# Sliding-window attention scores in half blocks: 64 queries of two heads against 192 keys

## The chip, the cores and the metric

The kernel runs on one core of a Trainium2 chip. The core has a matrix engine (PE, with a queue of its own for weight loads, PEld), a vector engine (DVE), an activation engine (ACT), a general engine (POOL) and a queue that issues transfers (SP), beside 16 DMA engines that do them. The metric is the device time of one execution in microseconds (us); before and after are compared by the median of several executions on the same chip.

## The reference

One layer of a decoder trunk: `x` is 2048 positions by 1024 channels, everything in 32-bit floats. The layer modulates `x` by a condition vector, projects it (`u @ w_in`) into queries, keys, values, an attention gate, a pool input, a pool gate and two merge gates, runs two mixers, projects and merges them, and ends in a layer norm. What the change touches is the first mixer:

```python
N_Q_HEADS, N_KV_HEADS, HEAD_DIM, WINDOW, BLOCK = 16, 2, 64, 128, 128

q_loc = jnp.arange(BLOCK)[:, None]
k_loc = jnp.arange(2 * BLOCK)[None, :]
dist = q_loc + BLOCK - k_loc
in_window = (dist >= 0) & (dist < WINDOW)
...
logits = jnp.einsum('bnqhgd,bnkhd->bnhgqk', qb, kb) * (HEAD_DIM ** -0.5) + bias
logits = jnp.where(mask, logits, NEG_INF)
probs = jax.nn.softmax(jnp.concatenate([logits, sink], axis=-1), axis=-1)[..., :-1]
out = jnp.einsum('bnhgqk,bnkhd->bnqhgd', probs, vb)
```

A block of 128 queries sees the 128 keys before the block and its own 128. Query number q of the block may use keys q+1 to q+128 of these 256. So each query uses 128 of the 256 keys; the first 64 queries of a block together use keys 1 to 191, the last 64 use keys 65 to 255. A learned bias by distance is added, and each head has a sink, one more logit that takes part in the softmax and is then dropped.

## The kernel before, in words

The kernel is one instruction stream per engine, in an order that the program writes down ahead of time (`keep_in_program_order`): no engine reorders, and each waits at its own place in line for the semaphores of others.

**The large products.** All projections are 1024-wide matrix products done by a Strassen-like scheme: seven products in place of eight, named `B11, T1, T2, B21, T3, B22, T4` after the tile set that they stream. Each is 12 matmuls of 128x512 (`product`, `mm3`: a high and a low part of both sides, three matmuls per 128 rows). A `Quad` is one such group of seven; its weights come from HBM into `W` and `A`, POOL forms sums of them, ACT rounds them to the high part (`w_set`), DVE forms the low part. `plan` fixes which product comes when, `run` walks them, and `consume` takes a finished product away: for queries (`q_quad`, line 576) ACT writes the high part `q_hi`, DVE the low part `q_lo`, and SP stores both into `q_d` in HBM two products later. Tiles for this come from a ring `c` of 4 (first half of the sequence) or 5 (second half).

**The stages.** The sequence is handled in two halves, s = 0 and 1, of 1024 positions. Each half has a start (`g0`, `g1`: keys, values, the first two query tiles, the first gates), a stage in which attention runs between the products (`o0`, `o1`), and an end (`e0`, `e1`: the pool mixer beside the last gates). A last stage (`mix`) does the output projections and the norm.

**Attention as an overlay.** `overlay` (line 769) cuts the attention of a half into 64 steps: 8 pairs of query heads (j) by 8 blocks of 128 positions. `beat` is called after every three matmuls of a product and lets a step in at a fixed rate, about one per 4.8 us. So where a step's PE work stands between the product's matmuls is fixed by the program. Step n does, in this order:

- PE: `scores(n)`, four matmuls 128x256 into the one bank `lg` (two heads, high and low part of the keys `kk`; the weights are 128 queries of one head, `qs`); `transposes(n-2)`, four transposes 128x128 into the one bank `pt`; `values(n-3)`, four matmuls 128x256 into `pv`.
- DVE and ACT: a reciprocal of the softmax sums of step n-1; two ACT operations that scale its probabilities by it; ACT copies `pt` to `pth` (rounded), and half of `pv` to `o`; per head, DVE adds the bias to `lg` and finds the row minimum in one operation (into the tile `L`), and ACT takes the exponential and its sum; DVE forms the low part `ptl`; two DVE adds finish the output block `st`.
- POOL: `new_l(n+1)` copies the two sinks into column 256 of each head's half of the next `L` tile (a ring of 3).

`lg` and `pt` exist once. So the scores of step n wait until DVE has read the `lg` of step n-1, and the transposes in step n wait until DVE has made the `ptl` of the step before.

**Transfers.** SP issues nearly all of them, in program order, with eight completion semaphores in turn. In the overlay it loads the queries of two blocks (`load_q`, line 796, two transfers of 128 KB) every second step, one pair ahead, and the bias of the next head pair (`load_bias`, line 805) once per 8 steps, into a tile `bt` of which there is one. The bias comes from `e_rep`, a copy of the per-head table for each of 128 partitions, read at a shifted offset per partition; `spread_bias` (line 766) writes these copies.

Of the kernel before, what the change touches and what calls it, by code (L numbers as in the profile page):

```python
# [15 lines left out]
ALU = mybir.AluOpType  # L16
# [43 lines left out]
def kernel(  # L60
# [30 lines left out]
    BF16 = mybir.dt.bfloat16  # L91
    set_names = ("B11", "T1", "T2", "B21", "T3", "B22", "T4")
# [7 lines left out]
    nsink = cp.tile([P, HEADS], F32, name="nsink")  # L100
# [7 lines left out]
    e_rep = dp.tile([P, HEADS, ET], F32, name="e_rep")  # L108
# [24 lines left out]
    q_d = dp.tile([2, KT, 2, 2, P, CH], F32, name="q_d")  # L133
# [632 lines left out]
    def spread_bias(j, q):  # L766
        q.dma_start(e_rep[:, 2 * j : 2 * j + 2, :], e_d[2 * j : 2 * j + 2, :].partition_broadcast(P))

    def overlay(ph, s, n_slots):
# [4 lines left out]
        kvt, qts, bts = {}, {}, {}  # L774
        marks, Es, Ls, pts, xs, pvs, outs, ags, kept = {}, {}, {}, {}, {}, {}, {}, {}, {}
# [20 lines left out]
        def load_q(h):  # L796
# [3 lines left out]
            q = qts[h] = tp.tile([P, 2, 2 * P], F32R, tag="qs", bufs=2, name="qs")  # L800
            for n in range(2):
                src = q_d[s, j, t, n][:, c * 2 * P : (c + 1) * 2 * P].rearrange("(h d) c -> d h c", h=2)
                sp.dma_start(as32(q[n * HD : (n + 1) * HD]), src)

        def load_bias(j):
            if j >= KT:
                return
            bt = bts[j] = tp.tile([P, 2, 2 * P], F32, tag="bt", bufs=1, name="bt")
            e_src = e_rep[:, 2 * j : 2 * j + 2, :]
            sp.dma_start(bt, bass.AP(e_src.tensor, e_src.offset + P - 1, [[HEADS * ET - 1, P], [ET, 2], [1, 2 * P]]))  # L810

        def new_l(n):
            if n < N:
                j = n // U
                room = tp.tile([P, 2 * 257 + 4], F32, tag="L", bufs=3, name="L")
                Ls[n] = room[:, 0 : 2 * 257].rearrange("p (h k) -> p h k", h=2)
                marks[n] = room[:, 2 * 257 : 2 * 257 + 2], room[:, 2 * 257 + 2 :]
                pool.tensor_copy(Ls[n][:, :, 256], nsink[:, 2 * j : 2 * j + 2])
# [4 lines left out]
        def values(n):  # L823
            k0 = k0_of(n)
            pv = pvs[n] = bank("pv")[:, 0 : 2 * P].rearrange("p (h q) -> p h q", h=2)
# [5 lines left out]
        def scores(n):  # L831
            k0, b, q = k0_of(n), n % U, qts[n // 2]
            lg = bank("lg").rearrange("p (h k) -> p h k", h=2)
            at = n % 2 * P
# [12 lines left out]
        def transposes(n):  # L847
            L = Ls.pop(n)
            pt = ps.tile([P, 2, 2, P], F32, tag="pt", bufs=1, name="pt")
            for hf in range(k0_of(n) // P, 2):  # L850
                for h in range(2):
                    pe.transpose(pt[:, hf, h, :], L[:, h, hf * P : (hf + 1) * P], ident)
# [21 lines left out]
        def step(n):  # L874
# [4 lines left out]
            if n - 1 in Es:  # L879
                E, e0, sm = Es.pop(n - 1)  # L880
                dve.reciprocal(sm, sm)
                for h in range(2):
                    act.activation(E[:, h, e0:256], E[:, h, e0:256], AF.Copy, scale=sm[:, h : h + 1])
# [10 lines left out]
            if lg is not None:  # L894
                j, e0 = n // U, k0_of(n)
                L = Ls[n]
                nm, sm = marks.pop(n)
                for h in range(2):
                    dve.tensor_tensor_reduce(
                        L[:, h, e0:256],  # L900
                        lg[:, h, e0:],
                        bts[j][:, h, e0:],
                        1.0,
                        nsink[:, 2 * j + h : 2 * j + h + 1],
                        ALU.add,
                        ALU.min,
                        nm[:, h : h + 1],
                    )
                    act.activation(
                        L[:, h, e0:257],  # L910
                        L[:, h, e0:257],
                        AF.Exp,
                        bias=nm[:, h : h + 1],
                        scale=-1.0,
                        accum_out=sm[:, h : h + 1],
                    )
                Es[n] = L, e0, sm
            if pt is not None:
                low(dve, lo[:, h0:], pt[:, h0:], hi[:, h0:])
            if o2 is not None:  # L920
# [7 lines left out]
                for h in range(2):  # L928
                    dve.tensor_tensor(
                        outs[jj, tt][h * HD : (h + 1) * HD, bb * P : (bb + 1) * P], pv[0:HD, h, :], o2[:, h, :], ALU.add  # L930
                    )
# [283 lines left out]
    def head(ph, grp):  # L1215
# [11 lines left out]

        dve.memset(as32(sets["B21"][:, 0, 0, :]), 1.0)
# [4 lines left out]
        act.dma_start(nsink, sinks.partition_broadcast(P))  # L1233
# [384 lines left out]
```

## Time and profile before

| | |
|---|---|
| median of 3 runs | 1700.26 us (1699.17 to 1703.98) |
| the profiled execution: its time, its span | 1703.35 us, 1701.2 us |
| mean granted PE clock | 0.993 |
| busy: PE, DVE, ACT, POOL | 1665.3, 1185.1, 988.4, 589.4 us |
| DMA: bytes moved, mean rate | 389.50 MB, 229 GB/s |
| the first overlay (s = 0) | about 160 to 476 us |
| the second overlay (s = 1) | about 742 to 1055 us |

Nearly every instruction goes through one helper line (`op(*args)`, line 56), so the profile's groups are told apart by tile names and shapes. `lg<-kk,qs` are the score matmuls, `pt<-ident,L` the transposes, `L<-lg,bt,nsink` the bias-and-minimum operation of DVE, `L<-L` on ACT with 257 columns the exponential and with 256 columns the scaling. With `set_...` and `w_set` as inputs a matmul belongs to a product, also where it writes `lg` or `c`. PE's busy time is modelled: an instruction counts until its results drain, so the busy time of one (`mean ns`) is longer than its share of a stream, and a stretch in which PE counts as busy may still hold short waits. The weight-load queue (PEld) shows such waits too.

### The profile page before, as it was taken

The page shows a single profiled execution, that of the slowest core. Times are in us where ns is not written, and L with a number is a line of the kernel's source. Part 1 is how long each engine was busy: PE and PEld are TensorE (multiplying, and loading weights), DVE is VectorE, ACT ScalarE, POOL GpSimd, SP SyncE. Part 2 cuts the span into 40 slices and gives each one's busy share as a digit, 9 for nine tenths or more (in the row PEclk, how much of TensorE's full clock was granted, in tenths as well). Part 3 has the DMA queues.
Part 4 walks back from the last instruction along what each step waited for, and adds up shares of the span by engine and source line. Part 5 has one row for each costly group of instructions (what it writes and reads, how often), then busy time and mean ns, then how long its engine had stood idle before and what let it go on. Part 6 is the DMA issues. An engine that isn't in the chain of part 4 may idle for free.

```text
span 1701.2 us, 24948 instructions
## 1 busy us (share of the span) xinstructions
PE 1665.3 (98%) x8112; PEld 1397.0 (82%) x8112; DVE 1185.1 (70%) x2167; ACT 988.4 (58%) x1943; POOL 589.4 (35%) x563
## 2 busy tenths in 40 slices
PE   9899999999999999999999999999999999999997
PEld 7788888888788888888888888888888888888886
DVE  6855666666647778656666666487876785778878
ACT  4645888787853336358877787333544453434553
POOL 3013454545462223323424333322242211113544
PEclk9899999999999999999999999999999999999999
DMA  9489676776557889865456454589968685777343
GB/s 358 151 294 311 202 225 217 242 239 208 170 178 223 264 288 326 289 206 157 150 171 215 156 175 135 190 280 326 329 238 309 197 312 201 261 264 281 149 149 124
DMA packets 236833, 389.50 MB, mean 229 GB/s; under 512 B 20872, under 2 KB 90528, under 8 KB 236576
## 3 DMA queue, kind: packets, MB, share of 16 engines
q1 hardware_dynamic: 231280, 382.36, 66.8%
q10 hardware_dynamic: 5392, 5.53, 1.0%
q8 instruction: 64, 1.05, 0.3%
q14 instruction: 65, 0.53, 0.1%
q0 software_dynamic: 32, 0.02, 0.0%
HBM read 243.63 MB, written 147.35 MB: 230 GB/s over the span
## 4 chain that ended last, share of the span: by engine, by line
PE 68%; ACT 11%; DVE 6%; issue 5%; DMA 3%; POOL 1%; SPq 1%; DVEq 0%; ACTq 0%; POOLq 0%
PE mm L56 43%; PE lg L56 11%; PE c L56 9%; ACT L L56 5%; PE pv L56 3%; PE pt L56 3%; DVE w_set L56 2%; ACT pth L56 2%; ACT w_set L56 1%; DVE wide L56 1%; ACT sig L56 1%; DVE p L56 1%; DVE ptl L56 1%; SPq L56 1%; ACT q_hi L56 0%
## 5 line engine op out<-in xcount | busy, mean ns | idle before, releaser
L56 PE MATMUL mm<-set_B,w_set 128*128 128x512 f32 x2664 | 652.7, 391 | 0.6 <-DVE w_set L56 0.6
L56 PEld LDWEIGHTS mm<-set_B,w_set 128*128 128x128 f32 x2664 | 496.6, 188 | 103.7 <-DVE w_set L56 1.5
L56 PE MATMUL mm<-set_T,w_set 128*128 128x512 f32 x1896 | 466.1, 392 | 1.5 <-POOL w_set L56 1.2
L56 POOL TENSOR_TENSOR W<-W 128x512 f32<-128x512 f32 x185 | 266.9, 1453 | 573.1 <-DVE w_set L56 394.0
L56 PEld LDWEIGHTS mm<-set_T,w_set 128*128 128x128 f32 x1896 | 351.5, 189 | 74.4 <-POOL w_set L56 2.5
L56 DVE TENSOR_TENSOR w_set<-W,w_set 128x1024 fp32r<-128x1024 f32 x197 | 254.5, 1292 | 110.5 <-ACT w_set L56 109.2
L56 ACT ACTIVATE L<-L 128x257 f32<-128x257 f32 (+3 forms) x512 | 241.4, 498 | 96.8 <-DVE L L56 96.3
L56 ACT CAST w_set<-W 128x1024 fp32r<-128x1024 f32 x222 | 232.2, 1047 | 97.2 <-PE mm L56 54.2
L56 PE MATMUL lg<-set_T,w_set 128*128 128x512 f32 x828 | 201.0, 391 | 2.7 <-ACT lg L56 1.7
L56 PE MATMUL c<-set_T,w_set 128*128 128x512 f32 x828 | 200.8, 391 | 0.0
L56 PEld LDWEIGHTS lg<-set_T,w_set 128*128 128x128 f32 x828 | 155.4, 188 | 36.2 <-ACT lg L56 2.1
L56 PEld LDWEIGHTS c<-set_T,w_set 128*128 128x128 f32 x828 | 155.8, 189 | 32.2
L56 DVE TENSOR_TENSOR ptl<-pt,pth 128x512 fp32r<-128x512 f32 (+1 forms) x128 | 86.4, 675 | 112.6 <-ACT pth L56 112.6
L56 POOL TENSOR_TENSOR W<-W,A 128x512 f32<-128x512 f32 x41 | 57.9, 1412 | 275.1 <-DMA A<-in_win_dram 102.7
L56 DVE CUSTOM_DVE_ANT_0 L<-lg,bt,nsink 128x256 f32<-128x256 f32 (+1 forms) x256 | 110.1, 467 | 25.1 <-PE lg L56 20.9
L56 ACT ACTIVATE sig<-mm 128x512 f32<-128x512 f32 x76 | 45.5, 599 | 94.6 <-PE mm L56 92.5
L56 PEld LDWEIGHTS lg<-kk,qs 128*128 128x128 f32 x512 | 77.4, 189 | 15.4 <-DVE L L56 4.6
L56 PE MATMUL pt<-ident,L 128*128 128x128 f32 x496 | 76.7, 276 | 9.3 <-DVE ptl L56 8.8
L56 PE MATMUL lg<-kk,qs 128*128 128x256 f32 (+1 forms) x512 | 81.5, 281 | 2.2 <-DVE L L56 1.9
L56 POOL TENSOR_TENSOR w_set<-W,w_set 128x1024 fp32r<-128x1024 f32 x25 | 61.0, 2441 | 63.7 <-ACT w_set L56 37.5
L56 PE MATMUL pv<-pth,vv 128*128 128x256 f32 x248 | 74.8, 323 | 1.1 <-DMA vv<-v_d 1.1
L56 DVE TENSOR_TENSOR st<-pv,o 64x128 f32<-64x128 f32 x256 | 71.3, 279 | 5.5 <-ACT o L56 3.8
(207 smaller groups left out, 1884.2 us busy)
## 6 DMA issues: line engine op xcount, KB each, us to landing
W<-in_win_dram SPq DMA_DIRECT2D x40, 512.0 KB, 5.8
qs<-q_d SPq DMA_DIRECT2D x128, 128.0 KB, 4.3
sums_d<-W SPq DMA_DIRECT2D x62, 256.0 KB, 4.1
W<-sums_d SPq DMA_DIRECT2D x31, 512.0 KB, 4.2
ain_d<-st SPq DMA_DIRECT2D x56, 256.0 KB, 3.5
A<-in_win_dram SPq DMA_DIRECT2D x42, 256.0 KB, 5.6
q_d<-q_hi SPq DMA_DIRECT2D x32, 256.0 KB, 4.4
q_d<-q_lo SPq DMA_DIRECT2D x32, 256.0 KB, 4.2
```

Of the source, the lines that this page charges most:

```text
L56: return lambda *args, **kw: self.tc.keep_in_program_order(op(*args, **kw))
```

## The change

Each step still handles one pair of heads and one block of 128 queries, with the same number of instructions. What lies on the 128 partitions differs: before, a score matmul had the 128 queries of one head; now it has 64 queries of both heads, first the early 64, then the late 64 (`eo` = 0, 1). For the early 64 only keys 0 to 191 are multiplied, biased and exponentiated, for the late 64 keys 64 to 255 (`span_of`). With it go:

- **Query layout.** `q_d` in HBM is now cut into pieces of 64 positions. A store (`keep_q`) writes 128 x 8 pieces of 64 numbers (256 bytes) where it wrote 128 rows of 512; a load reads 64 x 8 such pieces where it read 64 x 2 rows of 256 numbers (1 KB). The bytes are the same.
- **Bias.** A row of `bt` is now 192 numbers, the same for both halves up to a shift, for 64 partitions per head: two transfers of half the partitions, and two `bt` tiles in turn. `e_rep` has 64 copies in place of 128.
- **The L tiles** are three fixed tiles; the keys that no query of a half can use stay zero (three memsets on POOL at the start of each overlay), so that the transposes and the value matmuls keep their full width. The sinks stand in the column before the early half's keys and the column behind the late half's. `nsink` has one column per pair of heads.
- **Two more matmuls** of 128x512 (in `behind`): the bank `lg` is filled once at the start of `e0` and `e1`, as `c1` was already, since the scores no longer write all of it.

```diff
     class Pools:
         def __init__(self, name, **bufs):
             self.name, self.bufs, self.turns = name, {"c": 4, "p": 2, **bufs}, {}
-            self.fresh = True
+            self.fresh = {0, 1} if "pg" in bufs else {1}
...
-                if q.x and ph.fresh:
+                if q.pair and q.x in ph.fresh:
                     t = sets["B11"][:, 0, 0, :]
                     mm(q.c, t[:, 0:P], t, start=True, stop=True, skip_group_check=True)
-                    ph.fresh = False
+                    ph.fresh.remove(q.x)
...
+    def keep_q(dst, x):
+        sp.dma_start(dst.rearrange("b p c -> p b c"), x.rearrange("p (b c) -> p b c", c=HD))
...
-            defer(2 if m else 1, lambda: [sp.dma_start(q_d[s, m + mi, t, n], as32(x)) for n, x in enumerate((hi, lo))])
+            defer(2 if m else 1, lambda: [keep_q(q_d[s, m + mi, t, n], as32(x)) for n, x in enumerate((hi, lo))])
...
+        rooms = [tp.tile([P, 2 * 257 + 4], F32, tag=f"L{i}", bufs=1, name="L") for i in range(3)]
+        for room in rooms:
+            pool.memset(room[:, 1 + BAND : 1 + BAND + P], 0.0)
...
-            bt = bts[j] = tp.tile([P, 2, 2 * P], F32, tag="bt", bufs=1, name="bt")
-            e_src = e_rep[:, 2 * j : 2 * j + 2, :]
-            sp.dma_start(bt, bass.AP(e_src.tensor, e_src.offset + P - 1, [[HEADS * ET - 1, P], [ET, 2], [1, 2 * P]]))
+            bt = bts[j] = tp.tile([P, BAND], F32, tag="bt", bufs=2, name="bt")
+            for h in range(2):
+                e_src = e_rep[:, 2 * j + h, :]
+                at_q = bass.AP(e_src.tensor, e_src.offset + P - 1, [[HEADS * ET - 1, HD], [1, BAND]])
+                sp.dma_start(bt[h * HD : (h + 1) * HD], at_q)
...
+        def span_of(n, eo):
+            k0 = k0_of(n)
+            return (max(k0, HD), 2 * P) if eo else (k0, BAND)
...
-            for h in range(2):
+            for eo in range(2):
+                whi = q[:, n % 2 * 2 + eo].rearrange("p h c -> p (h c)")
+                k0, k1 = span_of(n, eo)
                 for hl in range(2):
                     mm(
-                        lg[:, h, k0:],
-                        q[:, h, at : at + P],
-                        kvt["k"][:, hl, (b - 1 + s) * P + k0 : (b + 1 + s) * P],
-                        start=h == 0 and hl == 0,
+                        lg[:, eo, k0:k1],
+                        whi,
+                        kvt["k"][:, hl, (b - 1 + s) * P + k0 : (b - 1 + s) * P + k1],
+                        start=eo == 0 and hl == 0,
                         stop=hl == 1,
                         skip_group_check=True,
                     )
...
-                for h in range(2):
-                    act.activation(E[:, h, e0:256], E[:, h, e0:256], AF.Copy, scale=sm[:, h : h + 1])
+                for eo in range(2):
+                    k0, k1 = span_of(n - 1, eo)
+                    x = E[:, 1 + 2 * P * eo + k0 : 1 + 2 * P * eo + k1]
+                    act.activation(x, x, AF.Copy, scale=sm[:, eo : eo + 1])
```

The order of all other instructions on every engine is as before. On SP, at the start of the first overlay, these are the rows before (rows read as: output, input, shape as partitions x pieces x numbers, and the semaphores waited for; `q_d` is the query store in HBM, `qs` the queries of two blocks, `e_rep` the bias copies, `A22`, `W` and `sums_d` weights and their kept sums):

```order
L56 DMA e_rep_77<-e_d_76 128x768 [waits DMAHW7_49,DMAHW5_49,DMASW0_49]
L56 DMA qs_1493<-q_d_89 64x2x256 [waits DMAHW6_49]
L56 DMA qs_1493<-q_d_89 64x2x256
L56 DMA q_d_89<-q_hi_1470 128x512 [waits DMAHW0_49,Activation_49]
L56 DMA q_d_89<-q_lo_1471 128x512 [waits DMAHW1_49,DVE_49]
L56 DMA A22_1515<-wmix_d_75 128x512 [waits DMAHW2_49,DVE_49]
L56 DMA sums_d_94<-W_1212 128x512 [waits DMAHW3_49,Pool_49]
L56 DMA q_d_89<-q_hi_1508 128x512 [waits DMAHW4_49,Activation_49]
```

and these are the same places now:

```order
L56 DMA e_rep_77<-e_d_76 64x768 [waits DMAHW1_49,DMAHW7_49,DMAHW0_49,DMASW0_49]
L56 DMA qs_1500<-q_d_89 64x8x64 x2
L56 DMA q_d_89<-q_hi_1477 128x8x64 [waits DMAHW2_49,Activation_49]
L56 DMA q_d_89<-q_lo_1478 128x8x64 [waits DMAHW3_49,DVE_49]
L56 DMA A22_1521<-wmix_d_75 128x512 [waits DMAHW4_49,DVE_49]
L56 DMA sums_d_94<-W_1213 128x512 [waits DMAHW5_49,Pool_49]
L56 DMA q_d_89<-q_hi_1514 128x8x64 [waits DMAHW6_49,Activation_49]
```

Nothing has changed places; the pieces of the query transfers are smaller and more, and the bias copies half as many.

On DVE, the second and third step of the first overlay read so before (`ISA` on `L<-lg,bt,nsink` is the bias-and-minimum operation, the row behind it reads its result out; `Pool_49` is POOL's sink copy into that `L`):

```order
L56 RECIPROCAL L_1496<-L_1496 128x2
L56 ISA L_1535<-lg_1567,bt_1393,nsink_71 128x256 [waits PE_49]
L56 ISA L_1535 128x1
L56 ISA L_1535<-lg_1567,bt_1393,nsink_71 128x256 [waits Pool_49]
L56 ISA L_1535 128x1
L56 TENSOR_TENSOR ptl_1579<-pt_1572,pth_1578 128x256 [waits Activation_49]
L56 RECIPROCAL L_1535<-L_1535 128x2 [waits Activation_49]
```

and now:

```order
L56 RECIPROCAL L_1389<-L_1389 128x2
L56 ISA L_1390<-lg_1572,bt_1400,nsink_71 128x192 [waits PE_49,Pool_49]
L56 ISA L_1390 128x1
L56 ISA L_1390<-lg_1572,bt_1400,nsink_71 128x192
L56 ISA L_1390 128x1
L56 TENSOR_TENSOR ptl_1584<-pt_1577,pth_1583 128x256 [waits DMAHW7_49,Activation_49]
L56 RECIPROCAL L_1390<-L_1390 128x2 [waits Activation_49]
```

The operations are a quarter narrower, and the wait for POOL's sink copy has moved from the second of the two to the first.

More of the change, by code (lines that the diff above doesn't have):

```diff
@@ L91 @@
     BF16 = mybir.dt.bfloat16
+    BAND = P + HD
     set_names = ("B11", "T1", "T2", "B21", "T3", "B22", "T4")
@@ L99 @@
     mod = cp.tile([P, 24], F32, name="mod")
-    nsink = cp.tile([P, HEADS], F32, name="nsink")
+    nsink = cp.tile([P, KT], F32, name="nsink")
     psc = cp.tile([P, KT], F32, name="psc")
@@ L107 @@
     e_d = dp.tile([HEADS, ET], F32, name="e_d")
-    e_rep = dp.tile([P, HEADS, ET], F32, name="e_rep")
+    e_rep = dp.tile([HD, HEADS, ET], F32, name="e_rep")
     gate_d = dp.tile([KT, P], F32, name="gate_d")
@@ L132 @@
     gates_d = {n: dp.tile([2, KT, 2, P, CH], F32, name=f"{n}_d") for n in ("ag", "pg", "ma", "mp")}
-    q_d = dp.tile([2, KT, 2, 2, P, CH], F32, name="q_d")
+    q_d = dp.tile([2, KT, 2, 2, CH // HD, P, HD], F32, name="q_d")
     k_d = dp.tile([2, P, 2, D], F32, name="k_d")
@@ L879, in step @@
             if n - 1 in Es:
-                E, e0, sm = Es.pop(n - 1)
+                E, sm = Es.pop(n - 1)
                 dve.reciprocal(sm, sm)
-                for h in range(2):
-                    act.activation(E[:, h, e0:256], E[:, h, e0:256], AF.Copy, scale=sm[:, h : h + 1])
+                for eo in range(2):
+                    k0, k1 = span_of(n - 1, eo)
+                    x = E[:, 1 + 2 * P * eo + k0 : 1 + 2 * P * eo + k1]
+                    act.activation(x, x, AF.Copy, scale=sm[:, eo : eo + 1])
             if pt is not None:
@@ L1232, in head @@
         act.dma_start(psc, pscale)
-        act.dma_start(nsink, sinks.partition_broadcast(P))
+        for h in range(2):
+            act.dma_start(nsink[h * HD : (h + 1) * HD, :], by_heads[h].partition_broadcast(HD))
         bias_rows()
```

61 lines of the change are left out of this document (31 added, 30 removed).

## The prediction, made before the changed kernel was run

> **What bounds the kernel now.** First the engines over the whole span and the chain of work that ended last (page, parts 1 and 4):
>
> ```profile
> PE 1665.3 (98%) x8112; PEld 1397.0 (82%) x8112; DVE 1185.1 (70%) x2167; ACT 988.4 (58%) x1943; POOL 589.4 (35%) x563
> PE 68%; ACT 11%; DVE 6%; issue 5%; DMA 3%; POOL 1%; SPq 1%; DVEq 0%; ACTq 0%; POOLq 0%
> ```
>
> PE bounds: it is busy for all but 36 us. Then the stages, of which the two overlays (second and third row) are where the change works:
>
> ```profile
> core 0: us, PE busy (x) PEld busy (x) DVE busy (x) ACT busy (x) POOL busy (x), PEclk, DMA share, GB/s
> 160.00:476.00 316.00, 307.38 (x1668) 261.40 (x1667) 201.95 (x588) 254.84 (x630) 158.04 (x176) 0.99 0.68 218
> 742.00:1055.00 313.00, 308.27 (x1704) 264.93 (x1702) 206.48 (x588) 250.14 (x617) 110.69 (x125) 1.00 0.53 172
> ```
>
> In them ACT is busy for 81% and DVE for 65%, and PE idles for 13.3 us in all. So DVE and ACT time is worth something only where PE waits for it. The list of waits has these for the two banks of the steps (columns: us in total, times, longest):
>
> ```profile
> PEld pt L56 <- DVE ptl L56: 14.5, 25, 0.9
> PEld lg L56 <- DVE L L56: 4.6, 8, 1.4
> ```
>
> 19.1 us in 33 waits: that is all that faster vector work can give back directly. The timeline shows one of the longest from inside:
>
> ```profile
> 453.73 0.15 DVE L56 RECIPROCAL L<-L 128x2 f32<-128x2 f32 x1
> 453.98 0.91 ACT L56 ACTIVATE L<-L 128x256 f32<-128x256 f32 x2 [2.06 <-DVE L L56]
> 454.20 0.47 DVE L56 CUSTOM_DVE_ANT_0 L<-lg,bt,nsink 128x256 f32<-128x256 f32 x1
> 454.79 0.57 ACT L56 CAST pth<-pt 128x512 fp32r<-128x512 f32 x1
> 455.39 0.69 DVE L56 TENSOR_TENSOR ptl<-pt,pth 128x512 fp32r<-128x512 f32 x1 [0.71 <-ACT pth L56]
> 456.14 0.33 PE L56 MATMUL pt<-ident,L 128*128 128x128 f32 x1 [0.67 <-DVE ptl L56]
> ```
>
> The transposes wait for a chain: reciprocal, two scalings on ACT (0.91 us), the copy `pth` (0.57), `ptl` on DVE (0.69). Of these only the scalings get shorter.
>
> **The change, term by term.** (a) *Score matmuls*, 192 columns in place of 256. Groups of four, in the timeline, wide and (at a block without earlier keys) narrow, each with what starts after it; and 16 matmuls of one column:
>
> ```profile
> 411.80 0.63 PE L56 MATMUL lg<-kk,qs 128*128 128x256 f32 x4
> 412.27 0.60 PE L56 MATMUL pt<-ident,L 128*128 128x128 f32 x4
> 161.69 0.63 PE L56 MATMUL lg<-kk,qs 128*128 128x128 f32 x4 [0.25 <-DMA qs<-q_d]
> 162.16 2.29 PE L56 MATMUL mm<-set_T,w_set 128*128 128x512 f32 x9
> 15.57 1.84 PE L56 MATMUL pt<-ct,head_T 128*128 128x1 f32 x16
> ```
>
> Four of 256 columns take 0.47 us to the next start, four of 128 columns also 0.47, and even with one column a matmul takes 1.84/16 = 0.115 us. So the load of new weights before each sets the pace, not the columns. Bounds for a group of 192: no gain, or by columns 0.47 x 1/4 = 0.12 us. It lies between 128 and 256, which are equal; I take 0.025 us (0.118 to 0.112 each), over 120 steps **-3 us**. The Trainium skill's page "TensorE: Matmul & The Clock Gate", section "Back-to-back issue gap", gives an isolated spacing that goes with the columns; by it the term would be about -13 us, and the equal rows above speak against it here.
>
> (b) *Vector work*, from the groups kept apart by shape (busy, mean ns):
>
> ```profile
> L56 ACT ACTIVATE L<-L 128x257 f32<-128x257 f32 x240 | 120.5, 505 | 2.8 <-DVE L L56 2.4 <-POOL L L56 0.4
> L56 ACT ACTIVATE L<-L 128x256 f32<-128x256 f32 x240 | 109.3, 504 | 86.7 <-DVE L L56 86.6
> L56 DVE CUSTOM_DVE_ANT_0 L<-lg,bt,nsink 128x256 f32<-128x256 f32 x240 | 105.2, 475 | 22.8 <-PE lg L56 18.6 <-POOL L L56 3.8
> L56 ACT ACTIVATE L<-L 128x129 f32<-128x129 f32 x16 | 6.3, 399 | 2.3 <-DVE L L56 2.3
> L56 ACT ACTIVATE L<-L 128x128 f32<-128x128 f32 x16 | 5.6, 397 | 5.1 <-DVE L L56 5.1
> L56 DVE CUSTOM_DVE_ANT_0 L<-lg,bt,nsink 128x128 f32<-128x128 f32 x16 | 4.9, 342 | 2.3 <-PE lg L56 2.3
> ```
>
> Busy time over count gives 0.502 and 0.394 us for the exponential, 0.455 and 0.350 for the scaling, 0.438 and 0.306 for the bias operation, at 256 and 128 columns. Halfway, at 192, they save 0.054, 0.053 and 0.066; two of each in a step: ACT -0.21, DVE -0.13 us per step, over 120 steps -26 and -16 us of busy time. That is cover for PE, not path. In a wait for `pt` the chain is 0.11 us shorter (two scalings), in a wait for `lg` 0.13: 25 x 0.11 + 8 x 0.13 = 3.8 us. A backlog carried over from the step before shrinks too, by up to the other 0.2 us; against that, PE comes a little earlier, and waits under 0.1 us give less. Bounds: 1 us, and two thirds of all 19.1 us. I take **-4 us**. What is late next in such a step is the product's own weight rounding in the same queues, which this doesn't touch.
>
> (c) *Two more matmuls* of 128x512, at 652.7/2664 = 0.245 us by the first row of the groups:
>
> ```profile
> L56 PE MATMUL mm<-set_B,w_set 128*128 128x512 f32 x2664 | 652.7, 391 | 0.6 <-DVE w_set L56 0.6
> ```
>
> **+0.5 us**. The three memsets on POOL stand ahead of the sums of the next weights, POOL being 35% busy: hidden. Without that cover each would be about a copy's length, well under 1 us. The moved wait (DVE's first bias operation for POOL's sink copy) costs where POOL is late; the row above counts 3.8 us of it, all of which the second operation waits for already, so at most one operation (0.44 us) more in the few such places, with `ptl` and `st` queued behind on DVE: within 1 us, taken as 0.
>
> (d) *Query transfers* in 256-byte pieces. DMA rows (queue: packets, MB, share of 16 engines; issues: count, KB, us to landing):
>
> ```profile
> q1 hardware_dynamic: 231280, 382.36, 66.8%
> q10 hardware_dynamic: 5392, 5.53, 1.0%
> qs<-q_d SPq DMA_DIRECT2D x128, 128.0 KB, 4.3
> q_d<-q_hi SPq DMA_DIRECT2D x32, 256.0 KB, 4.4
> q_d<-q_lo SPq DMA_DIRECT2D x32, 256.0 KB, 4.2
> ```
>
> A share of 16 x 1701.2 us over the packets gives 79 ns for a mean of 1653 bytes and 50 ns for 1026; the straight line has 15 ns at 256 bytes and 97 at 2 KB. A store had 8 packets per engine (0.78 us) and gets 64; a load had 8 (0.40 us) and gets 32. No group of 256-byte pieces stands in this profile, so: 15 ns from below, a 1 KB packet's 50 ns from above. I take 20, nearer the line: a store 1.28 us (+0.5), a load 0.64 (+0.24), so 64 and 128 of them +63 us on each engine; the lighter bias and its copies take off some 10. The mean share goes from 0.67 to 0.70, which binds nothing; but in places the DMA engines are full and PE is near a transfer:
>
> ```profile
> 90.00:96.00 6.00, 3.83 (x19) 2.99 (x18) 3.50 (x6) 3.32 (x6) 0.00 (x0) 0.94 1.03 329
> 162.00:168.00 6.00, 6.00 (x31) 5.01 (x30) 4.87 (x14) 3.25 (x10) 3.61 (x4) 1.00 1.07 375
> 744.00:756.00 12.00, 11.94 (x63) 9.98 (x62) 8.32 (x23) 7.51 (x21) 3.30 (x5) 1.00 0.93 325
> 94.96 2.66 PE L56 MATMUL pv<-spare,room_w 128*128 128x256 f32 x12 [2.17 <-DVE room_small L56]
> ACT room_small L56 <- DMA v_d<-room_small: 2.7, 1, 2.7
>   DMA q_d<-q_hi: 0.5, 1
> y_d<-wide SPq DMA_DIRECT2D x32, 256.0 KB, 6.9
> ```
>
> At 92 us ACT waits for the store `v_d`, and PE through DVE for ACT; ahead of `v_d` in the full queue go four query stores: 4 x 0.5 = 2, less some slack, +1.5. At 160 to 174 the first scores already wait 0.25 us for `qs`, and `q_hi` waits 0.5 us for a store of the ring `c` to land (last row but one, from the query tile's answer); two stores and two loads more costly, less the lighter bias: +1. At 744 to 756 the same with one ring tile more: +0.5. Together **+3 us**; bounds 0 (all hidden) and, at 50 ns a piece, 4 x 2.4 + 6 + 4 = 20.
>
> Sum: -3 - 4 + 0.5 + 3 = -3.5 us against the profiled execution's 1703.35 us (span 1701.2 and 2.15 around it), so 1699.9. The median shown is 3.1 us under that execution; on that scale the forecast is 1700.3 - 3.5 = **1697 us**, -0.2%. A measurement of this kernel tells about 0.3%, 5 us, from no change.
>
> **The rivals.** *The backlog clears*: DVE and ACT shed 0.34 us per step together and a wait is 19.1/33 = 0.58 us; if most waits hang on work left over from the step before, 13 of the 19.1 us go: -3 - 13 + 0.5 + 3 = -12.5, 1688 us. For it: ACT's 81%. Against: in the wait shown, DVE comes to the reciprocal late for a product's weights, not for a step's work.
>
> *The pieces cost as much as 1 KB packets* (slower side): 20 us by (d): -3 - 4 + 0.5 + 20 = +13.5, 1714 us. It decides from about 30 ns a piece on, where (d) reaches 7.5 us and eats (a) and (b). For it: the store `y_d<-wide` in the last row of (d)'s second fence has the bytes of a query store in 512-byte pieces and lands in 6.9 us for 4.4. Against: between the two queues packet time goes with the bytes, 0.048 and 0.049 ns each, and the `y_d` stores run in another stage. The Trainium skill's page "DMA: Bandwidth & Descriptors", section "Specifications", puts the smallest piece at line rate at 512 bytes and says that below it the engine reads, modifies and writes; that speaks for this case, and no row of this profile tests it.
>
> *Columns set the pace of the scores*: (a) is 0.12 x 120 = 14: -14 - 4 + 0.5 + 3 = -14.5, 1686 us. The equal groups of (a) speak against it.
>
> *Nothing comes of it*: the weight load holds (a) at 0 and PE, coming earlier, meets the same waits: about +0.5 + 3 - 3 of the shortest waits, 1700 us.
>
> **How the numbers follow.** Forecast 0.45 (own range 1691 to 1702), backlog 0.20, costly pieces 0.17, nothing 0.12, columns 0.06. Faster by over 0.3% (under 1695.2): 0.18 of the forecast's 0.45, 0.18 of the backlog's, 0.05 of the columns': 0.41. Slower by over 0.3% (over 1705.4): 0.15 of the costly pieces, 0.02 of the rest: 0.17. The remainder, 0.42, is no change. The range 1686 to 1709 takes in the backlog and half of the costly pieces and leaves out the far ends, some 0.17.
>
> **What would show it.** (a) A group of four 192-column scores takes 0.44 to 0.47 us to the next start; 0.35 would be the columns. (b) Bias operation 0.37, exponential 0.45, scaling 0.40 us; PEld's waits for `ptl` and `L` together 13 to 17 us (5 or less: the backlog). (c) `lg<-set_B` 51 times for 49. (d) Landing of the query stores 4.5 to 6 us, q1's share about 70%, PE's wait at 95 us 2 to 4 us; a share over 75% or waits of many us for `qs` or `q_hi` would be the costly pieces. The forecast is wrong if PE's waits in the overlays grow, or if the stages outside the overlays move by over 3 us.

## The result and the profile after

The changed kernel took 1711.26 us in the median (1710.21 to 1712.32, 4 runs) against 1700.99 us before (1699.17 to 1703.98, 4 runs, the same chip). The ratio is 1.0057, with a 95% interval of 1.0044 to 1.0069: slower by 10 us. The forecast was 1697, with a range of 1686 to 1709. Two executions far off the others (8382 us of k_wide below, 2368 us of the kernel before beside it) are left out of the ratios.

First the stages, from the changed kernel's timeline: the first and the last group of score matmuls of each overlay (columns: start us, us, engine, ..., number of matmuls, idle time before).

```profile
171.66 0.63 PE L56 MATMUL lg<-kk,qs 128*128 128x64 f32 x4 [1.40 <-DMA qs<-q_d]
472.83 0.59 PE L56 MATMUL lg<-kk,qs 128*128 128x192 f32 x4
748.80 0.66 PE L56 MATMUL lg<-kk,qs 128*128 128x192 f32 x4 [0.30 <-issue]
1050.01 0.59 PE L56 MATMUL lg<-kk,qs 128*128 128x192 f32 x4
```

and of the kernel before (its first group, at 161.69, stands in the prediction):

```profile
471.20 0.63 PE L56 MATMUL lg<-kk,qs 128*128 128x256 f32 x4
743.33 0.71 PE L56 MATMUL lg<-kk,qs 128*128 128x256 f32 x4
1049.50 0.63 PE L56 MATMUL lg<-kk,qs 128*128 128x256 f32 x4
```

By differences of these starts the overlays became shorter, 309.5 to 301.2 us and 306.2 to 301.2, so -13.3 together. Everything else became longer: +10.0 before the first scores, +3.8 between the overlays, and +8.8 behind the second one (the spans being 1701.2 and 1710.5). So the overlays gained about twice the 7 us that the forecast's (a) and (b) gave them, and stages that the change seems not to touch lost 22.6 us together.

**Where the first 10 us are.** The head of the changed program in windows of 4 us:

```profile
core 0: us, PE busy (x) PEld busy (x) DVE busy (x) ACT busy (x) POOL busy (x), PEclk, DMA share, GB/s
8.00:12.00 4.00, 4.00 (x26) 3.56 (x26) 1.37 (x3) 0.00 (x0) 0.00 (x0) 1.00 0.21 59
12.00:16.00 4.00, 1.70 (x8) 1.08 (x6) 1.36 (x3) 0.00 (x0) 0.00 (x0) 1.00 0.38 101
16.00:20.00 4.00, 0.00 (x0) 0.00 (x0) 0.15 (x1) 0.00 (x0) 1.09 (x7) 0.85 0.85 305
20.00:24.00 4.00, 0.89 (x5) 0.89 (x5) 2.10 (x4) 2.56 (x4) 4.00 (x15) 0.50 1.02 362
```

its timeline there: two weight loads on SP, POOL's first work on the bias table (`in_relT`), and PE's second group of one-column matmuls,

```profile
6.53 7.45 SPq L56 DMA_DIRECT2D W<-in_win_dram  x2
18.91 6.19 POOL L56 TENSOR_SCALAR head_T<-head_T 16x1 f32<-16x1 f32 x21 [17.25 <-DMA head_T<-in_relT_dram]
23.11 3.57 PE L56 MATMUL pt<-ct,head_T 128*128 128x1 f32 x16 [9.41 <-DMA head_T<-in_wadat_dram]
```

and the DMA rows of the sinks' load (count, KB each, us to landing) and of the queue that it is on:

```profile
nsink<-in_sinks_dram ACTq DMA_DIRECT2D x2, 2.0 KB, 13.4
q10 hardware_dynamic: 6176, 5.14, 0.9%
```

The kernel before, in the same windows,

```profile
8.00:12.00 4.00, 4.00 (x22) 3.51 (x23) 3.16 (x7) 0.23 (x1) 3.01 (x9) 0.75 1.04 409
12.00:16.00 4.00, 4.00 (x19) 3.28 (x17) 2.36 (x3) 2.33 (x4) 4.00 (x13) 0.83 1.03 404
```

and in the same rows of its timeline and of its DMA issues:

```profile
8.99 12.29 POOL L56 TENSOR_SCALAR head_T<-head_T 16x1 f32<-16x1 f32 x32 [7.33 <-DMA head_T<-in_relT_dram]
```

```profile
nsink<-in_sinks_dram ACTq DMA_DIRECT2D x1, 8.0 KB, 6.5
```

At 8 to 16 us the DMA engines were full before; after, they move 59 and 101 GB/s. SP hangs 7.45 us in the issue of two weight loads (1.08 before), POOL's bias work begins 10 us later, PE stands still for 9.41 us, and when it goes on, the granted clock is 0.50 (16 matmuls take 3.57 us for 1.84). What is new there is a piece of the change that the diff shown above leaves out: `nsink` now has one column per pair of heads, and its load changed with it. It was one transfer with 64 bytes for each of 128 partitions; it is two transfers that gather every second sink for 64 partitions each, 1024 pieces of 4 bytes:

```diff
-    nsink = cp.tile([P, HEADS], F32, name="nsink")
+    nsink = cp.tile([P, KT], F32, name="nsink")
...
+        by_heads = sinks.rearrange("(j h) -> h j", h=2)
...
-        act.dma_start(nsink, sinks.partition_broadcast(P))
+        for h in range(2):
+            act.dma_start(nsink[h * HD : (h + 1) * HD, :], by_heads[h].partition_broadcast(HD))
```

**Where the rest is.** In the output stage, where neither kernel does any attention, PE issues fewer matmuls in the same 200 us, and no idle time explains it. Before, then after, and the largest group of matmuls after:

```profile
1300.00:1500.00 200.00, 199.75 (x882) 165.13 (x881) 151.10 (x168) 83.45 (x98) 37.01 (x28) 1.00 0.73 251
```

```profile
1300.00:1500.00 200.00, 200.00 (x870) 162.89 (x869) 147.55 (x166) 84.60 (x99) 35.78 (x27) 1.00 0.73 254
```

```profile
L56 PE MATMUL mm<-set_B,w_set 128*128 128x512 f32 x2664 | 660.5, 394 | 0.7 <-DVE w_set L56 0.7
```

200 us over 882 is 226.8 ns a matmul, over 870 229.9, at a clock of 1.00 in both. The mean busy time of the largest group (394 ns) is up from the 391 of the prediction's row. Nothing of what these matmuls compute was changed. But `nsink` takes 32 bytes of each partition and not 64, and all that is allocated behind it lies 32 bytes lower: four of the seven token sets (`T4, T3, B22, T2`), `W`, and the weights `w_set`. They started at multiples of 64 bytes and now start 32 past one; the sets `B11, T1, B21` lie ahead of `nsink` and did not move.

Inside the overlays, the rows that answer to those of (a) in the timeline and of (b) in the groups by shape:

```profile
221.20 0.59 PE L56 MATMUL lg<-kk,qs 128*128 128x192 f32 x4
221.63 0.60 PE L56 MATMUL pt<-ident,L 128*128 128x128 f32 x4
```

```profile
L56 ACT ACTIVATE L<-L 128x193 f32<-128x193 f32 x240 | 107.6, 452 | 3.4 <-DVE L L56 3.4
L56 ACT ACTIVATE L<-L 128x192 f32<-128x192 f32 x240 | 96.3, 450 | 87.5 <-DVE L L56 87.2
L56 DVE CUSTOM_DVE_ANT_0 L<-lg,bt,nsink 128x192 f32<-128x192 f32 x240 | 89.7, 411 | 32.7 <-PE lg L56 22.8 <-POOL L L56 4.7 <-issue 2.7
```

The group of four scores takes 0.43 us for 0.47. The exponential is at 107.6/240 = 0.448 us, the scaling at 0.401, the bias operation at 0.374: as forecast.

### The profile page after: what moved, and what is told of

The parts are those of the page before. It is cut to its first block, busy times and chain, and to the rows that moved or that the text cites. A ratio compares the mean times of both kernels' runs of the same rounds, so it can differ in the third digit from the quotient of the medians.

```text
span 1710.5 us, 24915 instructions
## 1 busy us (share of the span) xinstructions
PE 1672.2 (98%) x8114; PEld 1389.5 (81%) x8114; DVE 1167.3 (68%) x2167; ACT 963.7 (56%) x1943; POOL 588.4 (34%) x569
## 3 DMA queue, kind: packets, MB, share of 16 engines
q1 hardware_dynamic: 335600, 378.56, 69.4%
## 4 chain that ended last, share of the span: by engine, by line
PE 78%; DVE 6%; ACT 6%; DMA 4%; issue 4%; SPq 1%; POOL 1%; DVEq 0%; ACTq 0%; POOLq 0%
PE mm L56 49%; PE lg L56 12%; PE c L56 9%; PE pv L56 3%; PE pt L56 3%; ACT L L56 2%; SPq L56 1%; DVE w_set L56 1%; ACT pth L56 1%; DVE wide L56 1%; DMA W<-in_wap_dram 1%; ACT w_set L56 1%; DVE ptl L56 1%; DMA qs<-q_d 1%; DVE p L56 1%
## 5 line engine op out<-in xcount | busy, mean ns | idle before, releaser
L56 PE MATMUL mm<-set_B,w_set 128*128 128x512 f32 x2664 | 660.5, 394 | 0.7 <-DVE w_set L56 0.7
L56 ACT ACTIVATE L<-L 128x193 f32<-128x193 f32 (+5 forms) x512 | 214.8, 446 | 98.7 <-DVE L L56 98.3
L56 DVE CUSTOM_DVE_ANT_0 L<-lg,bt,nsink 128x192 f32<-128x192 f32 (+2 forms) x256 | 94.0, 405 | 36.2 <-PE lg L56 26.3
L56 PE MATMUL lg<-kk,qs 128*128 128x192 f32 (+2 forms) x512 | 75.5, 269 | 3.0 <-DMA qs<-q_d 1.8
L56 ACT CAST pth<-pt 128x512 fp32r<-128x512 f32 (+1 forms) x128 | 71.9, 561 | 8.9 <-PE pv L56 7.8
```

The costliest lines, as they stand in the source:

```text
L56: return lambda *args, **kw: self.tc.keep_in_program_order(op(*args, **kw))
```

## The experiments

Each kernel ran beside the kernel before on the same chip; its time stands against that one's.

**Are these two the causes?** Four kernels: each cause taken out of the changed kernel alone, both taken out, and the move of 32 bytes alone put into the kernel before.

```diff
# a_align: the changed kernel
-    nsink = cp.tile([P, KT], F32, name="nsink")
+    nsink = cp.tile([P, HEADS], F32, name="nsink")[:, 0:KT]
# a_sinks: the changed kernel
-        by_heads = sinks.rearrange("(j h) -> h j", h=2)
+        by_heads = sinks.rearrange("(h j) -> h j", h=2)
...
-        "sinks": a["sinks"][0],
+        "sinks": a["sinks"][0].reshape(KT, 2).T.reshape(HEADS),
# a_both: both edits
# b_shift: the kernel before
-    mhalf = cp.tile([P, 1], F32, name="mhalf")
-    warm = cp.tile([P, 1], F32, name="warm")
+    mw = cp.tile([P, 2], F32, name="mhalf")
+    mhalf, warm = mw[:, 0:1], mw[:, 1:2]
```

> The changed kernel with one edit: the tile of sinks takes 16 columns again (64 bytes of a partition, as before the change) of which 8 are used, so that the token sets, the weight tiles and W, which the change moved by 32 bytes, start at multiples of 64 bytes again. Theory A (the operands' place in SBUF: product matmuls 512 wide are slower where their operands start at 32 past a multiple of 64): these matmuls fall from 394 back to 391 ns in the page's rows, their starts from about 230.4 to 227 ns apart outside the overlays, and the time falls by 15 to 18 us, to about 1694 (1692 to 1697). Rival B (the product matmuls are slower because the change's 256-byte pieces or its vector work disturb them): no difference, 1711 (within 2 us), the rows stay at 394.

> The changed kernel with one edit: the host hands the 16 sinks over ordered by head of a pair, so that each of their two loads reads rows of 32 bytes (64 of them) where it read 4-byte pieces (512 of them). Theory C (the head of the program is held up by these 1024 small pieces: the queues' other loads, W and relT, come late): POOL's wait for relT falls from 17.3 to 7 to 9 us, the first use of relT on POOL starts near 9 to 10 us rather than 18.9, and the time falls by 7 to 10 us, to about 1702 (1701 to 1704). Rival (the late head is absorbed by the stream of weights behind it, and the 10 us are all in the product matmuls): within 2 us of 1711.

> Both edits of a_align and a_sinks in the changed kernel. If the two causes are separate and complete, the gains add: 1711 - 17 - 9 = about 1685 (1682 to 1689), about 16 us faster than the kernel before, which is then what the change of scores alone is worth. If one of the causes is not what I take it for, the time is near that of the other edit alone (1694 or 1702). If the forecast's own sum for the edits of the scores (-3.6 us) was right, it is near 1697.

> The kernel before with one edit: two one-column tiles of 32 bytes, mhalf and warm, become one tile of two columns, so that everything allocated behind them (four of the token sets, W, the weight tiles, the overlays' pools) starts 32 bytes lower, at 32 past a multiple of 64, as in the changed kernel; nothing else differs. Theory A (place in SBUF): the product matmuls' rows go from 391 to 394 ns and the time from 1701 to 1715 to 1719. Rival B (the change's own work disturbs the products): no difference, 1701 (within 2 us).

| | median us (range) | ratio to before, 95% |
|---|---|---|
| a_align | 1697.15 (1694.64 to 1697.36) | 0.9965 (0.9952 to 0.9978) |
| a_sinks | 1702.48 (1698.09 to 1705.73) | 1.0004 (0.9993 to 1.0016) |
| a_both | 1688.28 (1686.58 to 1690.29) | 0.9919 (0.9903 to 0.9936) |
| b_shift | 1715.12 (1712.53 to 1718.14) | 1.0076 (1.0060 to 1.0092) |

Against the changed kernel's 1711.3 the place is worth 14.1 us, the sinks 8.8, both 23.0: they add. (The changed kernel's time is that of the result, measured apart from these four; by the ratios it is 15.7, 9.0 and 23.5, each with an error of some 3 us.) The stages agree: by the starts of the score groups a_align is back at 272.5 us between the overlays and 651.8 behind the second one (before 272.1 and 651.7, changed 276.0 and 660.5), and the first scores of a_sinks start at 160.1 us (before 161.7, changed 171.7). In b_shift the place alone costs 13.4 (before: 1701.71). With both causes out, the change is 13 us *faster* than before. In a_sinks POOL's wait is back:

```profile
9.45 13.17 POOL L56 TENSOR_SCALAR head_T<-head_T 16x1 f32<-16x1 f32 x32 [7.77 <-DMA head_T<-in_relT_dram]
8.34 2.48 PE L56 MATMUL pv<-ct,head_T 128*128 128x1 f32 x16 [0.80 <-DMA head_T<-in_wadat_dram]
```

**Do the 4-byte pieces do it alone?** In the kernel before:

```diff
# b_sinks: the kernel before
-        act.dma_start(nsink, sinks.partition_broadcast(P))
+        by_heads = sinks.rearrange("(j h) -> h j", h=2)
+        for h in range(2):
+            act.dma_start(nsink[h * HD : (h + 1) * HD, 0:KT], by_heads[h].partition_broadcast(HD))
+        act.dma_start(nsink[:, KT:], sinks[KT:].partition_broadcast(P))
```

> The kernel before with one edit: half of the sinks' tile is loaded by two DMAs of 4-byte pieces (512 each, as in the changed kernel), the other half by one DMA of 32-byte rows; the values get to other heads than they should, and only the time counts. If the pieces alone hold up the head of the program: POOL's wait for relT is 17 us and more, and the time 1709 to 1711. If they hold it up only together with something else of the change: 1701 to 1703.

Measured: 1710.63 us (1707.25 to 1711.08), ratio 1.0048 (1.0033 to 1.0064), so +9.3 us. The same wait is there:

```profile
19.20 5.84 POOL L56 TENSOR_SCALAR head_T<-head_T 16x1 f32<-16x1 f32 x19 [17.54 <-DMA head_T<-in_relT_dram]
```

The pieces are enough by themselves.

**Which operand's place is it?** The product matmuls have the weights `w_set` as their stationary operand and the token sets as the moving one. Two kernels move one side, then all:

```diff
# w_off: a_both
+            if "pad" not in phase_ps:
+                phase_ps["pad"] = wp.tile([P, 8], F32, name="pad")
             return wp.tile([P, D], F32R, tag="wset", bufs=4, name="w_set")
...
             self.t = self.stack.enter_context(tc.tile_pool(name=self.name, bufs=1, reuse_waits="tile"))
+            self.pad = self.t.tile([P, 8], F32, name="pad")
# all_off: a_both
+    cp.tile([P, 8], F32, name="pad")
     sets = {n: set_tile(n) for n in ("B11", "T1", "B21")}
```

> The kernel of a_both with one edit: 32 unused bytes ahead of the four w_set tiles (and 32 more at the head of each overlay's pool, so that the places there stay as they were), so that the weights, TensorE's stationary operand, start at 32 past a multiple of 64, and the token sets, its moving operand, stay at multiples of 64. In the changed kernel's mixing stage the starts of the matmuls come in blocks of twelve, one block for each token set: exactly 227 ns apart in some, about 234 in others, though all weights had moved and only four of seven sets. Theory M (the moving operand's place counts): no difference to a_both, 1688 (within 2.5 us). Rival W (the stationary operand's place counts): the cost of b_shift comes back, 1700 to 1704. Each by half: about 1695.

w_off took 1714.47 us (1712.82 to 1717.79), ratio 1.0080 (1.0060 to 1.0101): 26 us more than a_both. Neither theory had that. The cost is twice what rival W gave, though fewer tiles had moved than in the changed kernel. So I took the spacing apart by token set, from the start of one product matmul to the next behind 1060 us, matched with the program's order:

| mean ns to the next start | B11, T1, B21 | T4, T3, B22, T2 |
|---|---|---|
| a_both: all at 0 | 226.7 to 226.8 | 226.7 to 226.8 |
| changed kernel: weights at 32, these sets at | 0: 233.3 to 233.6 | 32: 226.8 to 229.7 |
| b_shift: weights at 32, these sets at | 0: 233.3 to 233.6 | 32: 226.8 to 229.6 |
| w_off: weights at 32, all sets at 0 | 233.2 to 233.4 | 233.2 to 233.3 |

(0 and 32: bytes past a multiple of 64.) Theory M had taken the slow sets for the four that moved: it is those that did *not* move. Slow is the matmul whose two operands stand differently. Hence the next test:

> The kernel of a_both with one edit: 32 unused bytes ahead of the first token set, so that all seven sets, W and the weights start at 32 past a multiple of 64 bytes (the overlays' own tiles change places from 32 to 0, so that their fifth w_set stands apart from the sets as it did). After w_off the place of one operand alone can't be the reason: there the sets stood at 0 and the weights at 32 and the time was 1714.5; in the changed kernel the three sets that had not moved with the weights (B11, T1, B21) are the slow ones, 233.4 ns a matmul, and the four at 32 with the weights take 227 to 229.7. Theory R (what counts is whether the moving and the stationary operand stand alike against 64 bytes): 1688 as a_both (within 2.5). Rival S (an operand at 32 past is slow whatever the other does): all products at 233 or more, 1712 to 1716.

all_off took 1685.69 us (1685.13 to 1686.73), ratio 0.9909 (0.9895 to 0.9922): with all operands at 32, nothing is lost, and by the same count every set takes 226.7 ns. Rival S falls, theory R holds for the two places that were tried. That 64 bytes is the measure, and not a larger step that a shift of 32 upsets as well, is not shown. The windows of the output stage say it too, w_off and then all_off:

```profile
1300.00:1500.00 200.00, 200.00 (x859) 161.06 (x858) 144.85 (x163) 84.54 (x99) 35.78 (x27) 1.00 0.72 249
```

```profile
1300.00:1500.00 200.00, 200.00 (x884) 165.69 (x883) 142.59 (x163) 84.00 (x101) 34.48 (x26) 1.00 0.70 240
```

232.8 ns a matmul against 226.2. Three of seven sets stand apart from the weights in the changed kernel: 26.2 x 3/7 = 11 us by w_off's cost, 14.1 measured; the set that follows a slow one needs some matmuls to be back at 227 (229.7 in the table), which is the likely rest.

**Does it reach into the overlays?** The overlays' own tiles stand at 32 in a_both, among them a fifth `w_set`.

```diff
# ov_align: a_both
-        rooms = [tp.tile([P, 2 * 257 + 4], F32, tag=f"L{i}", bufs=1, name="L") for i in range(3)]
+        rooms = [tp.tile([P, 528], F32, tag=f"L{i}", bufs=1, name="L")[:, 0 : 2 * 257 + 4] for i in range(3)]
```

> The kernel of a_both with one edit: the three L tiles of an overlay take 2112 bytes of a partition and not 2080, so that all that comes behind them there (kk, qs, vv, the fifth w_set, pth, ptl) starts at multiples of 64 bytes too. Theory M: moving operands there are kk in the scores, which the weight loads pace, and pth and ptl in the value products, 252 of 128x256; by half of the 7 ns of a 512 wide one that is at most 252 x 3.5 ns = 0.9 us: 1687 to 1688. If more of the overlays' 229.8 ns a matmul (against 227 elsewhere) comes from places in SBUF: up to 1800 x 2.8 ns = 5 us, 1683.

1688.18 us (1684.50 to 1692.04), ratio 0.9924 (0.9904 to 0.9943): no difference to a_both that can be told. From start to start the product matmuls of the two overlays take 230.1 and 229.8 ns in a_both and 229.8 and 229.7 in ov_align, against 226.7 behind them: what slows them there is not this, and stays open.

**What were the forecast's own terms worth?** (a) taken back in a_both, then (b) as well:

```diff
# k_wide: a_both, in scores
-                k0, k1 = span_of(n, eo)
+                k0, k1 = k0_of(n), 2 * P
# v_wide: k_wide
-            bt = bts[j] = tp.tile([P, BAND], F32, tag="bt", bufs=2, name="bt")
+            bt = bts[j] = tp.tile([P, 2 * P], F32, tag="bt", bufs=2, name="bt")
...
-                at_q = bass.AP(..., [[HEADS * ET - 1, HD], [1, BAND]])
+                at_q = bass.AP(..., [[HEADS * ET - 1, HD], [1, 2 * P]])
...
-            return (max(k0, HD), 2 * P) if eo else (k0, BAND)
+            return k0, 2 * P
...
-                        bts[j][:, k0 - HD * eo : k1 - HD * eo],
+                        bts[j][:, k0:k1],
```

> The kernel of a_both with one edit: the score matmuls compute all 256 keys (128 of the first block) as before the change, of which the vector work still uses 192; the transfers, the vector work and everything else are the changed ones. This is the part (a) of the forecast taken back. The forecast's term: 512 x 6 ns = +3 us, 1691. By the starts of the score matmuls in the changed kernel's trace (105 to 106 ns apart against 119): 512 x 13.5 ns = +7 us, 1695. If PE waits for the vector work there anyway: 1688.

> The kernel of k_wide (256 keys in the score matmuls) with the vector work back at 256 keys too: bias, exponential and scaling work on 128x256 (257 with the sink) again. For the second 64 queries of a block the bias is taken 64 columns off, so its values are wrong and only its time counts. This is part (b) of the forecast taken back. The forecast's term is 4 us (bounds 1 to 12.7), 1696 against k_wide's 1692. If all that a_both gained beside (a) is (b), as the waits ahead of PE in the overlays say (lg to pt 21 us in the trace of k_wide and 28 before): back to within 2 us of the kernel before, 1699 to 1703. If the gain was elsewhere (places, transfers): 1692.

k_wide took 1691.87 us (ratio 0.9944, 0.9926 to 0.9961), 3.6 over a_both. v_wide took 1703.34 us (1698.98 to 1706.11; ratio 1.0009, 0.9999 to 1.0020), 11.5 over k_wide and 2.0 over the kernel before. So (a) is about -3.6, (b) -11.5, and what is left, (c) and (d) in place, +2.0 (by the ratios: -4.2, -11.1, +1.5; the intervals allow an error of some 4, 3 and 2 us). By the starts of the score groups the two overlays together take 604.3 us in k_wide and 614.1 in v_wide, so nearly all of (b) is in them. The idle time ahead of the transposes, of PE and of its weight loads, shows where, k_wide and then v_wide (PE before: 9.3; the changed kernel: 5.3):

```profile
L56 PE MATMUL pt<-ident,L 128*128 128x128 f32 x496 | 75.5, 273 | 4.2 <-DVE ptl L56 4.0
L56 PEld LDWEIGHTS pt<-ident,L 128*128 128x128 f32 x496 | 56.7, 140 | 7.3 <-issue 3.7 <-POOL L L56 2.9
```

```profile
L56 PE MATMUL pt<-ident,L 128*128 128x128 f32 x496 | 76.0, 274 | 10.7 <-DVE ptl L56 9.7 <-POOL W L56 0.6
L56 PEld LDWEIGHTS pt<-ident,L 128*128 128x128 f32 x496 | 55.9, 140 | 16.2 <-POOL L L56 7.1 <-issue 6.3 <-POOL ux L56 0.8
```

**The small pieces by themselves.** (d) alone in the kernel before, and the number of its loads alone:

```diff
# b_pieces: the kernel before; q_d and its stores as in the changed kernel
-                src = q_d[s, j, t, n][:, c * 2 * P : (c + 1) * 2 * P].rearrange("(h d) c -> d h c", h=2)
-                sp.dma_start(as32(q[n * HD : (n + 1) * HD]), src)
+                for g in range(2):
+                    src = q_d[s, j, t, n, 4 * c : 4 * c + 4, g * HD : (g + 1) * HD, :].rearrange("b d c -> d b c")
+                    sp.dma_start(as32(q[n * HD : (n + 1) * HD, g]).rearrange("p (b c) -> p b c", c=HD), src)
# b_loads: the kernel before; the same two lines replaced
+                for g in range(2):
+                    src = q_d[s, j, t, n][g * HD : (g + 1) * HD, c * 2 * P : (c + 1) * 2 * P]
+                    sp.dma_start(as32(q[n * HD : (n + 1) * HD, g]), src)
```

> The kernel before with one edit: the queries are stored and loaded in pieces of 256 bytes, as in the changed kernel (the loads as 64 columns of four blocks, one for each head, so that there are 64 more of them than in the changed kernel; each query transfer's issue took SP 0.6 us or less). Scores, vector work and places in SBUF are those of before. This is the part (d) of the forecast alone: 3 us, 1704 (bounds: 1701.5 for no cost, 1714 for the rival that each small piece costs what a large one does). If (d) was the reason for the lost time after all, as that rival had it: 1712 to 1716.

> The kernel before with one edit: the query loads are issued for each head apart, 64 more of them and half as large, in the same pieces of 1 KB from the same rows. It tells how much of b_pieces' 8.5 us are its 64 more loads. If the pieces of 256 bytes are the reason: 1700 to 1702, as before, and part (d) of the forecast (3 us) was too small by 5 us. If the number of loads is: 1705 to 1709, and the pieces cost the 3 us of the forecast or less.

b_pieces took 1708.92 us (ratio 1.0050, 1.0032 to 1.0069), +8.5; b_loads 1704.59 (1.0020, 1.0006 to 1.0033), +3.2. So the pieces cost some 5 us there, between the two outcomes that I had written down, and the intervals just touch (an error of some 4 us). (The number in both expectations is half what it was: the trace counts 256 query loads for 128.) In b_loads PE waits 2.8 us at one place for the values (1.1 before), which SP loads too; that the added loads hold them up is likely and was not tried apart:

```profile
L56 PE MATMUL pv<-pth,vv 128*128 128x256 f32 x248 | 74.8, 323 | 2.8 <-DMA vv<-v_d 2.8
```

## Why the prediction was wrong

The sum lacked two terms, and one of its own was too small:

| term | forecast | measured | from |
|---|---|---|---|
| (a) score matmuls | -3 | -3.6 | k_wide - a_both |
| (b) vector work | -4 | -11.5 | v_wide - k_wide |
| (c), (d) matmuls, transfers | +3.5 | +2.0 | v_wide - before |
| operands apart by 32 bytes | not there | +14.1 | changed - a_align |
| sinks in 4-byte pieces | not there | +8.8 | changed - a_sinks |
| sum | -3.5 | +9.8 | result: +10.3 |

**The step that failed** is the inventory of the change: "The change, term by term" follows the arithmetic of the scores and leaves out `nsink`, its size and its load (the words of the change name its new column, the sum has no term for it). The forecast named the sign of it ("wrong ... if the stages outside the overlays move by over 3 us"; they moved by 22.6), but no rival had that cause.

**(a)** fits in size: k_wide gives 3.6, though its error of some 4 us does not exclude nothing. By the starts the gain is larger: in 0.43 us for 0.47 a group there are 120 x 0.04 = 5 us, just outside the 0.44 to 0.47 that were to show it; that part of it is given back, because PE comes to the next waits earlier, is likely and not shown. By the isolated spacing in the Trainium skill's page "TensorE: Matmul & The Clock Gate", section "Back-to-back issue gap", an estimate is about 13; k_wide disagrees.

**(b)** had the right durations and the right place, and a wrong size: 11.5 for 4. It took the chain in each of 33 waits as 0.11 to 0.13 us shorter and bounded the backlog by two thirds of 19.1 = 12.7. That was too little: with each step 0.34 us lighter on DVE and ACT, the idle time ahead of the transposes falls from 10.7 to 4.2 us on PE and from 16.2 to 7.3 us in its weight loads, two to three times what 0.11 us in each of the 25 waits for `ptl` would give. So work left over from the step before, which the forecast held to the smaller part, is the likely reason, as the rival *the backlog clears* had it; its -12.5 (with (a) to (d)) lies within the error of a_both's -13.4. No run takes the backlog and the chain apart. The sign that the forecast named for the backlog, 5 us or less in PEld's waits for `ptl` and `L`, came out (2.2 us in the changed kernel), but it cannot be leaned on: v_wide, with the wide vector work, shows 5.4, since most waits there go by another name (`POOL L`, `issue`).

**(c)** as forecast: `lg<-set_B` stands 51 times.

**(d)** had the price of a piece right and its effects in part: q1's share is 69.4% (70 forecast), the 256-byte packets took 19.7 ns in the mean (20 taken), and the first scores wait 1.40 us for `qs` where they waited 0.25. But the stores land in 4.3 and 4.2 us, as before (4.5 to 6 forecast), and PE's wait behind `v_d`, from which half of the 3 us was to come, is 1.8 us (2.2 before). The rows of the queue and of the stores, and the list of waits:

```profile
q1 hardware_dynamic: 335600, 378.56, 69.4%
q_d<-q_hi SPq DMA_DIRECT2D x32, 256.0 KB, 4.3
q_d<-q_lo SPq DMA_DIRECT2D x32, 256.0 KB, 4.2
```

```profile
ACT q_hi L56 <- DMA q_d<-q_hi: 4.8, 2, 3.9
```

ACT's waits for the ring of query tiles grew (last row, 4.8 us in two waits; 0.5 before). That all of this costs little is shown only together with (c) and the rest of the change: +2.0 us, with an error of some 2. The rival *the pieces cost as much as 1 KB packets* gave 1714, near the result, for a reason that is not there: with the pieces left in and the two other causes out, a_both runs at 1688.

## What to carry to other kernels

Read every line of a diff for what it does to memory: a tile that shrinks moves all that is allocated behind it, and a rearranged load may fall into 4-byte pieces. When stages slow down that a change does not touch, look at addresses too, and test it by moving them alone (pad or merge a tile). And where a queue may carry a backlog, a shorter operation can be worth more than its share of the waits' last links: here 11.5 us for the 3.8 that those links gave.

## What the runs showed of the hardware

- A stream of 128x512 matmuls ran at 226.7 ns from start to start where moving and stationary operand stood alike against 64 bytes of a partition (both at 0, or both at 32 past), and at 233.3 where one stood 32 past: 2.9%, and 26 us of this kernel where all weights stood apart (w_off). Why, and whether other distances matter, was not tried.
- The records of the 1024 pieces of 4 bytes show 7 to 9 ns each, but their starts are spread: four fifths lie between 6.7 and 15.8 us, some 55 for each of 16 engines, so about 0.17 us apart, and all transfers together fell from 409 to 59 GB/s at 8 to 12 us. With 128 rows of 32 bytes in their place (a_sinks) it was 376 GB/s there. The 256-byte pieces of the queries took 19.7 ns each, so 13 bytes per ns where the 1 KB packets of the same run carried 20 (51.4 ns each), and the query stores landed no later. The Trainium skill's page "DMA: Bandwidth & Descriptors", section "Specifications", says that below 512 bytes the engine reads, modifies and writes. The pieces of 4, 32 and 256 bytes are all below that, and the rate collapsed only around those of 4; whether that rule is the reason was not tried.
- After PE's pause of 9.41 us the clock was granted at 0.50. The 0.85 of the window from 16 to 20 us puts its fall at 18.8 us, some 5 us after the last matmul had ended at 13.7. The Trainium skill's page "TensorE: Matmul & The Clock Gate", section "Part 1: The HAM clock gate", halves the clock after an idle window of about 3.4 us; the trace agrees in this place. The kernel before has 0.75 and 0.83 at 8 to 16 us with PE counted as busy throughout, which no pause explains.
